# Eight PSUM banks shared out anew between scores, transposes and dense products, with P's products a step later

## The chip, the cores and the metric

The kernel runs on one core of a Trainium2 chip. A time is the device time of one execution in microseconds; fewer is better. TensorE (PE in the profile, with its weight loads as PEld) writes its products into PSUM, whose eight banks hold 128 x 512 numbers of 32 bits each; VectorE (DVE), ScalarE (ACT) and GpSimd (POOL) work beside it, SyncE (SP) issues most DMAs. Engines run their own streams and wait for one another through semaphores.

## The reference

Two layers on 1024 tokens of width 1024. Each has 16 attention heads of three kinds side by side, then a SwiGLU block and a gated per-layer input.

```python
for i in range(DEPTH):                      # DEPTH = 2
    hn = rms_norm(h, attn_norm[i])
    proj = hn @ w_in[i]                     # split into all queries, keys, values
    ...
    blocks = lax.map(lambda q0: mixer_block(q0, ...), starts)
    h = h + mix @ w_o[i]
    hf = rms_norm(h, ffn_norm[i])
    h = h + (jax.nn.silu(hf @ w_gate[i]) * (hf @ w_up[i])) @ w_down[i]
    g = jax.nn.sigmoid(rms_norm(h, ple_norm[i]) @ w_ple_gate[i])
    h = h + g * (p[i] @ w_ple_proj[i])
return rms_norm(h, final_norm)
```

`mixer_block` does for 128 queries:

```python
s = einsum('bqhd,bkhd->bhqk', q, mla_k) * scale       # 6 latent heads: causal softmax
o_mla = einsum('bhqk,bkhd->bqhd', softmax(s), mla_v)
ilog = einsum('bqhd,bkd->bqhk', idx_q, idx_k) * IDX_DIM ** -0.5
isc = einsum('bqhk,bqh->bqk', relu(ilog), idx_w)      # the indexer, 8 heads
_, sel = lax.top_k(isc, topk)                         # 256 keys for each query
...                                                   # 5 sparse heads: softmax over sel, with a bias
l1m = where(strict, log_sigmoid(-z), 0.0)             # 5 stick-breaking heads
w = where(strict, exp(log_sigmoid(z) + suffix), 0.0)
```

## The kernel before

**Tiling.** The tokens are two halves of 512. Features lie on the partitions. A dense product is 128 features by 512 tokens; every operand is a high and a low part, so each step of `gemm` (L259) over 128 inputs is three matmuls of 128x512: high by high, high by low, low by high (L266, L267, L268). ScalarE makes a weight's high part `wh` (L187), GpSimd its low part `wl` (L196).

**Two streams.** `weave` runs a main stream of dense work (in-projection, then `layer_rest`: output projection, SwiGLU, gate) and feeds a side stream, `attention(L, half)`, into it by a planned ratio. The attention of a half runs beside the dense work of the half or layer before it: (0,0) beside the in-projection's end, (0,1) beside `layer_rest(0,0)`, (1,0) beside `layer_rest(0,1)`, (1,1) beside `layer_rest(1,0)`; `layer_rest(1,1)` has nothing beside it. On TensorE instructions run in the order in which the program is written. The other engines' order is set by a scheduler by priority, with instructions that empty PSUM banks ahead.

**PSUM.** Four pools share the eight banks: `psS` (scores S, two banks to a tile, two tiles), `psT` (transposes T), `psO` (products with the values O) and `psD` (dense products D, two tiles). A tile taken again waits for the instruction that reads it last. Dense products are read by VectorE and ScalarE at L433, L508, L522, L554, L582, L616, L630, L656, L671, L1195 and L1197. T is read by L293, L344, L352, L367, L415 and by the heads' L835 and L836.

**Attention.** First the indexer: eight heads, each with a call of `scores` (L776) for every block of 128 queries (two blocks in the first half, four in the second), read by a relu on ScalarE (L1042). Then five stick-breaking heads, six latent, five sparse. While the first eleven run, VectorE also does the 32 rounds of counts of the top-k (L1082). A head has two chunks of 256 queries; a chunk of `n` pairs of key blocks runs through steps (L1122 to L1182):

- three and two steps before `s0`, `scores` of its two query blocks; in the step's second part `post_scores` reads S: two sigmoids on ScalarE (L886, L887) and a scan on VectorE (L888) for stick-breaking, VectorE's maximum (L867) and ScalarE's exp (L874) for latent, a masked maximum on VectorE (L870) for sparse;
- at `s0 + jp`, `piece(jp)`: up to four 128x128 transposes of P into T (L828); `post_piece` (L830) then has ScalarE copy T to PT's high part (L835) and VectorE subtract that for PT's low part (L836). PT has two buffers;
- a step later `pv(jp)` (L838): four matmuls of the values with PT's high and low parts into O (L845);
- after the last, `finish` (O read at L853 and L854), and at a head pair's end `norm` (L931), whose four transposes of `wide` (L941) lay the softmax row scales out in PSUM, with `scale` (L947) and `store`.

Here n is 1 and 2 in the first half (three steps to a head) and 3 and 4 in the second (seven). Within a step the order on TensorE is pv, norm, piece, scores (the table `order`), then the dense products that the ratio gives. A step's length in dense work follows from `weights`, from the number of things in it.

Of the kernel before, what the change touches and what calls it, by code (L numbers as in the profile page):

```python
# [8 lines left out]
F32 = mybir.dt.float32  # L9
# [12 lines left out]
HALF = 512  # L22
# [18 lines left out]
NORM_LATER = 1  # L41
# [6 lines left out]
STEP_W, STEPS = (4.0, 1.0), (220, 380)  # L48
SPARSE_W = 1.0
# [39 lines left out]
def trunk(ctx: ExitStack, tc, x, p, w_in, attn_norm, mla_q_norm, mla_w_uq, mla_kv_norm, mla_w_ukv,  # L89
# [5 lines left out]
    def pool(name, bufs=1, **kw):  # L95
        return ctx.enter_context(tc.tile_pool(name=name, bufs=bufs, **kw))
# [4 lines left out]
    ap = pool("ap", 1)  # L101
    sm = pool("sm", 4)
    PS = bass.MemoryType.PSUM
    psS, psT, psO, psD = pool("psS", 2, space=PS), pool("psT", 1, space=PS), pool("psO", 1, space=PS), pool("psD", 2, space=PS)
    dram = pool("dram", 1, space=bass.MemoryType.DRAM)

    def scratch(name, *shape):
# [2 lines left out]
    def S_tile():  # L110
        return psS.tile([128, 2, HALF], F32, name="S")

    def T_tile():
        return psT.tile([128, HALF], F32, name="T")

    def D_tile():
        return psD.tile([128, HALF], F32, name="D")
# [409 lines left out]
    def layer_rest(L, half):  # L527
# [179 lines left out]
                after(12 + 2 * i, lambda i=i: piece(i % 4, i // 4, T_tile))  # L707
            return
        norm.rstd()
        tiles = [S_tile()[:, i] for _ in range(2) for i in range(2)]  # L710
        tiles += [T_tile(), psO.tile([128, HALF], F32, name="O"), D_tile(), D_tile()]
        for i in range(8):
            piece(i % 4, i // 4, lambda: tiles[i])

# [1 line left out]
    def attention(L, half):  # L716
        k = (L, half)
        nk = HALF * (half + 1)
        tiles = [4 * half + i for i in range(4)]
        itiles = [t for t in tiles if t >= 2]  # L720
        off, o = {}, 0
        for t in itiles:
            off[t] = o
            o += 128 * (t + 1)
        isc = ap.tile([128, 3328], F32, name="isc")

        def have(*keys):
            return all(clock[0] - stored.get(key, 1e9) >= DELAY for key in keys)
# [47 lines left out]
        def scores(t, qs, ks, extra=None):  # L776

            n = 128 * (t + 1)
            w = max(n, 256)
            np_, w = (1, w) if w <= 512 else (2, w // 2)  # L780
            ql = (t % 4) * 128
            S = S_tile()
            for i in range(np_):
                mms = [(S[:, i, :w], a[:, ql:ql + 128], b[:, i * w:i * w + w]) for a, b in zip(qs, ks)]
                if i == np_ - 1 and extra is not None:
                    mms[1:1] = extra(t, S[:, i], n - i * w)
                for j, (o, a, b) in enumerate(mms):
                    PE.matmul(o, a, b, start=j == 0, stop=j == len(mms) - 1)  # L788
            if np_ == 1:
                return S[:, 0, :n], lambda a: a[:, :n], AX.X  # L790
            return S[:, :, :w], lambda a: a[:, :n].rearrange("p (a w) -> p a w", a=2), AX.XY

        def masked(mask):
            return lambda t, S, e: [(S[:, e - 128:e], identB, mask)]

# [9 lines left out]
        class Chunk:  # L805
# [8 lines left out]
            def scores(self, q):  # L814
                self.S[q] = scores(2 * self.c + q, *self.head.qk())
# [88 lines left out]
        class Head:  # L904
# [26 lines left out]
            def norm(self):  # L931

                j = self.i // 2
                if self.done and j in rows:
                    self.n = n = 64 if self.i % 2 == 0 else 128
                    self.S = S_tile()[:, 0]
                    wide = sm.tile([128, 4, 2, 64], F32, name="wide", bufs=1)
                    ACT.copy(wide[:, :, :n // 64], rows[j].rearrange("p h t -> p t h")[:, :, :n // 64].unsqueeze(
                        3).to_broadcast([128, 4, n // 64, 64]))
                    for t in range(4):  # L940
                        PE.transpose(self.S[:n, t * 128:(t + 1) * 128],  # L941
                                     wide[:, t, :n // 64].rearrange("p h c -> p (h c)"), identF)
# [89 lines left out]
        def indexer():  # L1032
# [27 lines left out]
            for hh in range(IDX_H):  # L1060
                qs = nxt()
                while hh + 1 < IDX_H and not have(("iq", k, (hh + 1) // 2)):
                    yield None
                for i, t in enumerate(itiles):
                    S, view, _ = scores(t, (qs, qs), (kh, kl))
                    accumulate(hh, t, S, view)
                    if i == 0 and hh + 1 < IDX_H:
                        nxt = load(hh + 1)
                    yield 0.5 + (t + 1) * 0.5
# [52 lines left out]
        post, prod = {}, {}  # L1122

        def at(d, step, f, *a):
            d.setdefault(step, []).append((f, a))

        load, first_sparse, nb = {}, None, 3 + 4 * half
        s0 = LAG[half] + 2
        for hd in heads:
            for ci, ch in enumerate(hd.chunks):  # L1130
                lag = LAG[half]
                if ci == 0:
                    at(load, s0 - lag - 2, hd.fetch)
                    at(load, s0 - lag - 1, hd.split)
                    at(load, s0 - 3, hd.fetch_values)
                    at(load, s0 - 1, hd.split_values)
                    if hd.kind is SparseHead and first_sparse is None:
                        first_sparse = s0 - lag + 1
                for q in range(2):
                    at(prod, s0 - lag + q, ch.scores, q)  # L1140
                    at(post, s0 - lag + q + 1, ch.post_scores, q)
                for jp in range(ch.n):
                    at(prod, s0 + jp, ch.piece, jp)
                    at(post, s0 + jp + 1, ch.post_piece, jp)
                    at(prod, s0 + jp + 1, ch.pv, jp)
                at(post, s0 + ch.n + 1, ch.finish)
                if ci == 1:
                    at(prod, s0 + ch.n + NORM_LATER - 1, hd.norm)
                    at(post, s0 + ch.n + NORM_LATER, hd.scale)
                    at(post, s0 + ch.n + NORM_LATER, hd.store)  # L1150
                s0 += ch.n

        order = {"finish": 0, "scale": 1, "store": 2, "post_piece": 3, "post_scores": 4, "pv": 5, "norm": 6, "piece": 7,
# [1 line left out]
        background = topk()  # L1155
        tk = TOPK_W[half] / max(first_sparse - 1, 1)
        credit = 0.0
        weights = [(STEP_W[0] + STEP_W[1] * len(prod.get(step, []))) * (1.0 if step < first_sparse else SPARSE_W) for step in range(s0 + 4)]
        unit = STEPS[half] / sum(weights)
        for step in range(s0 + 4):  # L1160
            for f, a in sorted(prod.get(step, []), key=lambda fa: order[fa[0].__name__]):
                f(*a)
            for f, a in load.get(step, []):
                while f.__name__ == "fetch" and not have(*f.__self__.needs()):
                    yield None
                f(*a)
            if step + 1 == first_sparse:
                for _ in background:
                    pass
            for f, a in sorted(post.get(step + 1, []), key=lambda fa: order[fa[0].__name__]):  # L1170
                f(*a)
            credit += tk * (TOPK_RATE[0] if step < SB_H * nb else TOPK_RATE[1])
            last = next((i for i in reversed(nc.cur_bb.bb.instructions) if i.engine == DVE.engine), None)
            with tc.issue_after(last):
                while credit > 0:
                    credit -= next(background, 1e9)
            yield weights[step] * unit
# [50 lines left out]
    def heads_of_all():  # L1228
        for L in range(DEPTH):
            for half in range(2):  # L1230
                yield from attention(L, half)
                ended.append((L, half))

    side = heads_of_all()
    parts = ((first, (), "in"), (layer_rest, (0, 0), "full"), (layer_rest, (0, 1), "full"), (layer_rest, (1, 0), "last"))
    for i, (f, a, name) in enumerate(parts):
        weave(f(*a), side, DENSE[name], ATT[i], lambda: len(ended) > i, clock)
    for _ in layer_rest(1, 1):
        pass
# [59 lines left out]
```

## Time and profile before

| | us |
|---|---|
| three runs: lowest, median, highest | 3209.86, 3210.99, 3216.07 |
| the profiled execution | 3211.26 |
| its span, first to last instruction | 3209.1 |
| attention (0,0): indexer, products with values | 56 to 99, 119 to 423 |
| attention (0,1) | 437 to 599, 627 to 1275 |
| attention (1,0) | 1292 to 1353, 1387 to 1797 |
| attention (1,1) | 1884 to 2033, 2062 to 2698 |
| top-k counts of the four | 104 to 286, 606 to 946, 1358 to 1569, 2042 to 2392 |

The mean granted clock of TensorE is 0.987. In a row of the grouped view stand line, engine, operation, output tile and inputs, shapes and count; behind the bar the busy time in total in us, the mean in ns, and the idle time of the engine just before the group in us, with the instructions that ended it. In the order of time, a row has its start and length in us, and in brackets the idle time before it.

### The profile page before, as it was taken

The page shows a single profiled execution, that of the slowest core. Times are in us where ns is not written, and L with a number is a line of the kernel's source. Part 1 is how long each engine was busy: PE and PEld are TensorE (multiplying, and loading weights), DVE is VectorE, ACT ScalarE, POOL GpSimd, SP SyncE. Part 2 cuts the span into 40 slices and gives each one's busy share as a digit, 9 for nine tenths or more (in the row PEclk, how much of TensorE's full clock was granted, in tenths as well). Part 3 has the DMA queues.
Part 4 walks back from the last instruction along what each step waited for, and adds up shares of the span by engine and source line. Part 5 has one row for each costly group of instructions (what it writes and reads, how often), then busy time and mean ns, then how long its engine had stood idle before and what let it go on. Part 6 is the DMA issues. An engine that isn't in the chain of part 4 may idle for free. (4 is left out here: it accounts for less than half of the span.)

```text
span 3209.1 us, 43576 instructions
## 1 busy us (share of the span) xinstructions
PE 3068.6 (96%) x15059; PEld 2549.1 (79%) x15059; DVE 2099.0 (65%) x3701; ACT 1486.3 (46%) x2485; POOL 1722.9 (54%) x1980
## 2 busy tenths in 40 slices
PE   8889999999998999999999999889999999999998
PEld 7768888777887888888888788767888877888877
DVE  4878656799997646687744636899997465322234
ACT  4555654445445545444444535544444455322234
POOL 4533356666445433765555744656445445766665
PEclk9999999999999999999999999999999999999999
DMA  7465453323233346433333465422333323333322
GB/s 203 117 194 147 144 172 96 91 89 96 90 97 93 105 116 176 132 103 107 107 104 89 116 162 176 116 72 86 98 97 95 89 70 113 117 99 94 98 92 73
DMA packets 549949, 363.59 MB, mean 113 GB/s; under 512 B 134672, under 2 KB 491744, under 8 KB 549728
## 3 DMA queue, kind: packets, MB, share of 16 engines
q1 hardware_dynamic: 549727, 360.81, 38.7%
q8 instruction: 119, 1.95, 0.3%
q14 instruction: 103, 0.84, 0.1%
HBM read 310.65 MB, written 50.08 MB: 112 GB/s over the span
## 5 line engine op out<-in xcount | busy, mean ns | idle before, releaser
L196 POOL TENSOR_TENSOR wl<-wr,wh 128x256 fp32r<-128x256 f32 x1684 | 1375.4, 848 | 1178.5 <-ACT wh L187 1143.9
L266 PE MATMUL D<-act,wh 128*128 128x512 f32 x3416 | 1363.6, 399 | 31.6 <-DVE h L582 16.5
L267 PE MATMUL D<-act,wh 128*128 128x512 f32 x3416 | 1341.0, 393 | 2.3 <-DVE act L633 2.0
L268 PE MATMUL D<-act,wl 128*128 128x512 f32 x3416 | 1340.0, 392 | 2.4 <-POOL wl L196 2.4
L266 PEld LDWEIGHTS D<-act,wh 128*128 128x128 f32 x3416 | 646.0, 189 | 174.7 <-issue 14.1
L268 PEld LDWEIGHTS D<-act,wl 128*128 128x128 f32 x3416 | 645.3, 189 | 145.9 <-POOL wl L196 4.8
L187 ACT CAST wh<-wr 128x1024 fp32r<-128x1024 f32 (+3 forms) x432 | 443.6, 1027 | 665.6 <-PE D L267 525.5
L267 PEld LDWEIGHTS D<-act,wh 128*128 128x128 f32 x3416 | 646.6, 189 | 126.6 <-DVE act L633 3.1
L1082 DVE TENSOR_SCALAR_CACHE_REDUCE junk<-isc,cand 128x512 uint8<-128x512 f32 (+5 forms) x396 | 371.3, 938 | 5.5
L836 DVE TENSOR_TENSOR PT<-T,PT 128x384 fp32r<-128x384 f32 (+1 forms) x320 | 201.8, 631 | 139.9 <-ACT PT L835 138.9
L835 ACT CAST PT<-T 128x384 fp32r<-128x384 f32 (+1 forms) x320 | 173.6, 542 | 192.4 <-PE T L828 181.4
L845 PEld LDWEIGHTS O<-PT,V 128*128 128x128 f32 x1280 | 196.2, 190 | 72.2 <-DVE PT L836 43.7
L845 PE MATMUL O<-PT,V 128*128 128x256 f32 x1280 | 215.5, 287 | 38.1 <-DVE PT L836 34.3
L891 POOL TENSOR_TENSOR P<-P,A 128x127 f32<-128x127 f32 (+3 forms) x80 | 101.0, 1266 | 198.3 <-DVE A L888 122.1
L788 PE MATMUL S<-kh,qh 128*128 128x384 f32 (+4 forms) x544 | 206.6, 381 | 0.3 <-ACT P L1042 0.3
L788 PE MATMUL S<-kl,qh 128*128 128x384 f32 (+4 forms) x544 | 203.8, 375 | 1.6 <-DVE kl L293 1.6
L828 PE MATMUL T<-identF,P 128*128 128x128 f32 x1152 | 182.2, 277 | 17.5 <-POOL P L891 6.6
L828 PEld LDWEIGHTS T<-identF,P 128*128 128x128 f32 x1152 | 135.4, 142 | 21.9 <-POOL P L891 9.0
L1048 DVE SCALAR_TENSOR_TENSOR isc<-P,iw,isc 128x384 f32<-128x384 f32 (+2 forms) x84 | 97.0, 1157 | 78.4 <-ACT P L1042 78.3
L619 POOL TENSOR_TENSOR tmp<-tmp,rr 128x512 f32<-128x512 f32 x88 | 120.2, 1366 | 32.4 <-DVE tmp L618 27.0
L630 DVE SCALAR_TENSOR_TENSOR tmp<-tmp,D 128x512 f32<-128x512 f32 x88 | 60.1, 683 | 107.6 <-POOL tmp L619 80.3
L853 ACT COPY o<-O 64x256 f32<-64x256 f32 x128 | 47.3, 370 | 175.4 <-PE O L845 174.0
(217 smaller groups left out, 3304.4 us busy)
## 6 DMA issues: line engine op xcount, KB each, us to landing
wr<-in_w_gate_dram SPq DMA_DIRECT2D x88, 512.0 KB, 3.8
wr<-in_w_up_dram SPq DMA_DIRECT2D x88, 512.0 KB, 3.8
wr<-in_w_down_dram SPq DMA_DIRECT2D x80, 512.0 KB, 3.4
wr<-in_w_in_dram SPq DMA_DIRECT2D x44, 512.0 KB, 3.8
wr<-in_w_in_dram SPq DMA_DIRECT2D x76, 256.0 KB, 3.8
wr<-in_w_o_dram SPq DMA_DIRECT2D x32, 512.0 KB, 4.3
wr<-in_w_ple_gate_dram SPq DMA_DIRECT2D x32, 512.0 KB, 3.8
h<-h SPq DMA_DIRECT2D x56, 256.0 KB, 4.4
```

The costliest lines, as they stand in the source:

```text
L187: ACT.copy(hi, raw)
L196: POOL.tensor_tensor(l[:, ks], a[:, ks], f32(h[:, ks]), op=ALU.subtract)
L266: PE.matmul(ps, a, ah, start=first and i == 0, stop=False)
L267: PE.matmul(ps, a, al, start=False, stop=False)
L268: PE.matmul(ps, b, ah, start=False, stop=last and i == len(ks) - 1)
L619: POOL.tensor_tensor(t, t, ffn.rep, op=ALU.mult)
L788: PE.matmul(o, a, b, start=j == 0, stop=j == len(mms) - 1)
L828: PE.transpose(ps[:, o:o + 128], self.P[q][:, j * 128:(j + 1) * 128], identF)
L835: ACT.copy(pt[:, 0, o:], self.ps[:, o:])
L836: DVE.tensor_sub(pt[:, 1, o:], self.ps[:, o:], f32(pt[:, 0, o:]))
L845: PE.matmul(self.O[:, :256], self.head.V[:, j, :], pt[:, s, o:o + 256], start=j == 0 and s == 0, stop=j == 2 * self.n - 1 and s == 1)
L1082: DVE.tensor_scalar(junk[:, :n], isc[:, off[t]:off[t] + n], c[:, i:i + 1], None, op0=op, op1=ALU.add, accum_out=cnt[:, i:i + 1])
```

## The change

One pair of S banks instead of two, two T banks instead of one, three D banks instead of two; O keeps its one. In the first half an attention takes the S pair once and holds it, and each call of `scores`, which there needs one bank, uses the pair's two banks in turn (`S_banks`); in the second half a call takes the pair as before. The head's row scales are laid out in a T tile instead of S. `pv`, `finish`, `norm`, `scale` and `store` come one step later, so an attention has one step more. The output's last eight pieces take their banks in another division. From L732 on, a line's number in the changed kernel is 9 higher.

```diff
-    psS, psT, psO, psD = pool("psS", 2, space=PS), pool("psT", 1, space=PS), pool("psO", 1, space=PS), pool("psD", 2, space=PS)
+    psS, psT, psO, psD = pool("psS", 1, space=PS), pool("psT", 2, space=PS), pool("psO", 1, space=PS), pool("psD", 3, space=PS)
...
-        tiles = [S_tile()[:, i] for _ in range(2) for i in range(2)]
-        tiles += [T_tile(), psO.tile([128, HALF], F32, name="O"), D_tile(), D_tile()]
+        S = S_tile()
+        tiles = [S[:, 0], S[:, 1], T_tile(), T_tile(), psO.tile([128, HALF], F32, name="O"), D_tile(), D_tile(), D_tile()]
...
+        if half == 0:
+            own, uses = S_tile(), [0]
+
+        def S_banks():
+
+            if half:
+                return S_tile()
+            uses[0] += 1
+            return own[:, uses[0] % 2:uses[0] % 2 + 1]
...
-            S = S_tile()
+            S = S_banks()
...
-                    self.S = S_tile()[:, 0]
+                    self.S = T_tile()
...
-                    at(prod, s0 + jp + 1, ch.pv, jp)
-                at(post, s0 + ch.n + 1, ch.finish)
+                    at(prod, s0 + jp + 2, ch.pv, jp)
+                at(post, s0 + ch.n + 2, ch.finish)
                 if ci == 1:
-                    at(prod, s0 + ch.n + NORM_LATER - 1, hd.norm)
-                    at(post, s0 + ch.n + NORM_LATER, hd.scale)
-                    at(post, s0 + ch.n + NORM_LATER, hd.store)
+                    at(prod, s0 + ch.n + NORM_LATER, hd.norm)
+                    at(post, s0 + ch.n + NORM_LATER + 1, hd.scale)
+                    at(post, s0 + ch.n + NORM_LATER + 1, hd.store)
...
-        for step in range(s0 + 4):
+        for step in range(s0 + 5):
```

What moves on TensorE, first in a stick-breaking chunk of the second layer's second half. T_20363 is P's transposes of one piece, and PT_20374 is made from it; before, its product stands at the next step, with 18 dense matmuls between (left out but for one):

```order
L828 MATMUL T_20363<-identF_84,P_20096 128x128
L828 MATMUL T_20363<-identF_84,P_20160 128x128
...
L788 MATMUL S_20368<-kl_20262,qh_20258 128x384
L266 MATMUL D_20236<-act_19988,wh_20239 128x512
...
L845 MATMUL O_20289<-PT_20374,V_20045 128x256 x4
L828 MATMUL T_20445<-identF_84,P_20096 128x128
```

Now, at such a place, with T_20311 and PT_20322 made from it, the preceding piece's product (PT_20257) and the next piece's transposes (T_20359) come in between:

```order
L837 MATMUL T_20311<-identF_84,P_20145 128x128
L837 MATMUL T_20311<-identF_84,P_20212 128x128
...
L797 MATMUL S_20316<-kl_20075,qh_20071 128x448
...
L854 MATMUL O_20193<-PT_20257,V_19887 128x256 x4
L837 MATMUL T_20359<-identF_84,P_20145 128x128
...
L797 MATMUL S_20364<-kl_20075,qh_20071 128x512
...
L854 MATMUL O_20434<-PT_20322,V_20254 128x256 x4
L837 MATMUL T_20439<-identF_84,P_20145 128x128
```

The product moved behind a second stretch of dense work; 39 dense matmuls now stand between the transposes and it.

Second, the indexer's calls of scores in the first half of the first layer, two rows to a call, with the semaphores of other engines that a row waits for (Activation is ScalarE); dense matmuls lie between the calls. Before, each call has a tile of its own, in two pairs of banks, and the third call is the first that waits for ScalarE:

```order
L788 MATMUL S_725<-kh_668,qh_722 128x384
L788 MATMUL S_725<-kl_669,qh_722 128x384
...
L788 MATMUL S_740<-kh_668,qh_722 128x512
L788 MATMUL S_740<-kl_669,qh_722 128x512
...
L788 MATMUL S_784<-kh_668,qh_781 128x384 [waits Activation_49]
L788 MATMUL S_784<-kl_669,qh_781 128x384
...
L788 MATMUL S_807<-kh_668,qh_781 128x512 [waits Activation_49]
```

Now all calls write the one tile S_447, in its two banks by turns:

```order
L797 MATMUL S_447<-kh_669,qh_723 128x384
L797 MATMUL S_447<-kl_670,qh_723 128x384
...
L797 MATMUL S_447<-kh_669,qh_723 128x512 [waits Activation_49]
L797 MATMUL S_447<-kl_670,qh_723 128x512
...
L797 MATMUL S_447<-kh_669,qh_780 128x384 [waits Activation_49]
L797 MATMUL S_447<-kl_670,qh_780 128x384
```

The wait for ScalarE has moved from the third call to the second.

Third, a pair of latent heads' end in the first layer's second half, where the row scales go into PSUM just ahead of a piece's transposes. Before:

```order
L941 MATMUL S_9889<-identF_84,wide_9890 128x128 x4
L828 MATMUL T_9896<-identF_84,P_9715 128x128
L828 MATMUL T_9896<-identF_84,P_9770 128x128
...
L788 MATMUL S_9901<-kh_9658,qh_9654 128x448
L788 MATMUL S_9901<-kl_9659,qh_9654 128x448
```

Now:

```order
L950 MATMUL T_9848<-identF_84,wide_9849 128x128 x4
L837 MATMUL T_9855<-identF_84,P_9618 128x128
L837 MATMUL T_9855<-identF_84,P_9678 128x128
...
L797 MATMUL S_9860<-kh_9557,qh_9553 128x512
L797 MATMUL S_9860<-kl_9558,qh_9553 128x512
```

They moved from S to T, where the piece's transposes follow at once.

More of the change, by code (lines that the diff above doesn't have):

```diff
@@ L1157, in attention @@
         credit = 0.0
-        weights = [(STEP_W[0] + STEP_W[1] * len(prod.get(step, []))) * (1.0 if step < first_sparse else SPARSE_W) for step in range(s0 + 4)]
+        weights = [(STEP_W[0] + STEP_W[1] * len(prod.get(step, []))) * (1.0 if step < first_sparse else SPARSE_W) for step in range(s0 + 5)]
         unit = STEPS[half] / sum(weights)
-        for step in range(s0 + 4):
+        for step in range(s0 + 5):
             for f, a in sorted(prod.get(step, []), key=lambda fa: order[fa[0].__name__]):
```

## The prediction

> **What bounds the kernel now.** I read the page's busy times first, then TensorE's rows grouped by line, then its waits in the stretches where VectorE is busiest, then the order of time around one wait.
>
> ```profile
> span 3209.1 us, 43576 instructions
> PE 3068.6 (96%) x15059; PEld 2549.1 (79%) x15059; DVE 2099.0 (65%) x3701; ACT 1486.3 (46%) x2485; POOL 1722.9 (54%) x1980
> ```
>
> TensorE is busy for 3068.6 of 3209.1 us, the next engine for 65%. The 140 us between are all that a new sharing of PSUM can win, save for the clock (below). The grouped rows end with the idle time ahead of a group and what ended it:
>
> ```profile
> L266 PE MATMUL D<-act,wh 128*128 128x512 f32 x3416 | 1363.6, 399 | 31.6 <-DVE h L582 16.5 <-DVE stg L508 3.8 <-DVE tmp L630 3.4
> L845 PE MATMUL O<-PT,V 128*128 128x256 f32 x1280 | 215.5, 287 | 38.1 <-DVE PT L836 34.3 <-DVE nm L872 1.6 <-DVE mix L854 1.1
> L828 PE MATMUL T<-identF,P 128*128 128x128 f32 x1152 | 182.2, 277 | 17.5 <-POOL P L891 6.6 <-DVE rr L367 2.9 <-DVE act L293 2.3
> L341 PE MATMUL T<-ones,rr 128*128 128x1 f32 x160 | 20.7, 250 | 11.5 <-DVE rr L323 6.9 <-DVE PT L836 4.6
> L413 PE MATMUL T<-identF,stg 128*128 128x128 f32 x96 | 15.0, 280 | 4.5 <-DVE PT L836 2.9 <-DVE stg L433 1.6
> L1188 PE MATMUL D<-identF,act 128*128 128x128 f32 x64 | 13.7, 346 | 10.1 <-DMA act<-in_x_dram 7.3 <-DVE stg L522 1.2 <-ACT h L1195 1.0
> L360 PE MATMUL T<-identF,rstd 128*128 128x128 f32 x80 | 12.6, 281 | 10.1 <-DVE rstd L352 8.2 <-DVE PT L836 1.9
> L941 PE MATMUL S<-identF,wide 128*128 128x128 f32 (+1 forms) x96 | 14.4, 272 | 0.0
> ```
>
> The costliest wait is of the products with the values (O) for PT, P's transposed copy; next is a dense product (D) for the instruction that still reads its bank (h, stg, tmp); then transposes (T), partly for the last reader of the one T bank. These are the three things that the change touches. Two stretches in which VectorE also does the top-k counts, and their shares (columns: us, busy time of PE, PEld, DVE, ACT, POOL, then granted clock, DMA share, GB/s):
>
> ```profile
> PE O L845 <- DVE PT L836: 11.8, 10, 3.1
> PE D L266 <- DVE h L582: 4.9, 4, 2.3
> PE D L266 <- DVE tmp L630: 2.1, 1, 2.1
> ...
> PE O L845 <- DVE PT L836: 20.0, 14, 3.9
> PE T L360 <- DVE rstd L352: 8.2, 1, 8.2
> PE D L266 <- DVE h L582: 3.2, 2, 1.9
> ...
> 600.00:700.00 100.00, 91.17 (x451) 75.06 (x450) 99.09 (x154) 48.56 (x70) 61.58 (x62) 0.98 0.30 92
> 700.00:800.00 100.00, 93.01 (x479) 77.12 (x478) 99.03 (x154) 50.97 (x75) 63.67 (x63) 1.00 0.31 95
> 2100.00:2200.00 100.00, 92.00 (x452) 76.22 (x451) 92.32 (x143) 49.31 (x73) 57.48 (x58) 0.95 0.28 85
> 2200.00:2300.00 100.00, 94.80 (x486) 78.95 (x485) 96.81 (x163) 48.92 (x75) 55.24 (x58) 0.98 0.31 93
> 2900.00:3000.00 100.00, 99.81 (x441) 82.35 (x440) 26.03 (x36) 25.40 (x30) 64.93 (x80) 1.00 0.32 95
> ```
>
> The first three wait rows are of 600 to 960 us, the next three of 2040 to 2440: in the second alone lie 20.0 of the 38.1 us before O. Where no attention runs (2900 to 3000) TensorE is full at 99.81 of 100.
>
> **The change part by part.** No instruction is added or removed; banks and one step of time move.
>
> *The products a step later.* The dearest wait in order of time:
>
> ```profile
> 2119.99 3.38 DVE L888 TENSOR_TENSOR_SCAN A<-A,zeros 128x1024 f32<-128x1024 f32 x1
> ...
> 2121.78 0.49 PE L828 MATMUL T<-identF,P 128*128 128x128 f32 x3
> 2124.18 0.39 PE L266 MATMUL D<-act,wh 128*128 128x512 f32 x1
> 2124.41 0.39 PE L267 MATMUL D<-act,wh 128*128 128x512 f32 x1
> 2125.54 0.28 PE L845 MATMUL O<-PT,V 128*128 128x256 f32 x1
> 2128.48 0.54 DVE L836 TENSOR_TENSOR PT<-T,PT 128x384 fp32r<-128x384 f32 x1
> 2129.08 0.62 PE L845 MATMUL O<-PT,V 128*128 128x256 f32 x3 [3.27 <-DVE PT L836]
> ...
> 2131.21 0.63 PE L267 MATMUL D<-act,wh 128*128 128x512 f32 x1
> 2131.64 0.63 PE L268 MATMUL D<-act,wl 128*128 128x512 f32 x1
> 2134.32 0.64 PE L845 MATMUL O<-PT,V 128*128 128x256 f32 x4
> ```
>
> The transposes end at 2122.3, the dense work between is used up by 2125.54, and the subtraction that makes PT's low part is held up behind a scan and other VectorE work until 2129.02. A step later the product stands where the next one does now: 2134.32, or 2131.05 without the 3.27 us of wait. That is 2.0 us behind the subtraction. So this wait goes, with a margin shorter than the wait was. In the second half the example of the change's order has 39 dense products where 18 stood, about 9 us of cover against 4. I take all of O's 38.1 us but the 1.1 that waits for `mix` (O's own bank, still one, still one step): **37**.
>
> *A third D bank.* Then a product waits for the reader of the bank three products back. By the trace each such reader had ended at least 0.5 us before its bank would come round in the old order. Of L266's 31.6 us the row names 23.7, all readers of D; I leave 2.4 out for what it doesn't name, and add 2.8 of L1188 (10.1 less 7.3 for the DMA): **32**.
>
> *A second T bank.* The waits for PT (4.6 + 2.9 + 1.9), for stg (1.6, which reads the bank as well) and L828's but for P (17.5 - 6.6 = 10.9) are for T's reader; with two banks the trace leaves 1.6 us of margin at the closest. I count the first three and the last: **20**. What waits for data stays: rr L323 6.9, rstd 8.2, P 6.6, the DMA 7.3. Together 37 + 32 + 20 = 89.
>
> *The clock.* Behind the wait at 2129 the dense products start 0.43 us apart where 0.23 was usual before it (2131.21 to 2131.64; 2124.18 to 2124.41). The granted clock there:
>
> ```profile
> 2131.00:2133.50 2.50, 2.50 (x7) 1.92 (x7) 2.50 (x7) 0.63 (x1) 0.93 (x2) 0.50 0.63 179
> 2425.00:2427.00 2.00, 2.00 (x6) 1.71 (x6) 1.46 (x2) 0.38 (x1) 0.00 (x0) 0.50 0.00 0
> 2422.78 0.62 PE L845 MATMUL O<-PT,V 128*128 128x256 f32 x3 [1.87 <-DVE PT L836]
> ```
>
> About 3.4 us at 0.50 lose 1.7 us; ten such stretches stand behind waits counted above, and since part of a stretch falls on the wait itself I take 1.2 us each: **12** more.
> [...]
>
> *One pair of S banks.* This costs. In the second half a call of scores now waits for the reader of the call just before:
>
> ```profile
> 82.00 0.33 PE L788 MATMUL S<-kh,qh 128*128 128x384 f32 x1
> 84.08 0.48 PE L788 MATMUL S<-kh,qh 128*128 128x512 f32 x1
> 86.06 0.62 ACT L759 CAST qh<-qraw 128x512 fp32r<-128x512 f32 x1 [4.78 <-DMA qraw<-iq]
> 86.59 0.49 ACT L1042 ACTIVATE P<-S 128x384 f32<-128x384 f32 x1
> ...
> 912.31 1.01 ACT L874 ACTIVATE P<-S,nm 128x896 f32<-128x896 f32 x1 [4.42 <-DVE nm L867]
> 913.33 0.48 PE L788 MATMUL S<-kh,qh 128*128 128x512 f32 x1
> ```
>
> The last two rows are one of the closest: read out at 913.32, next call at 913.33. Over the second half's calls one of 192 comes out late, by 0.3 us, and four more are within 0.5. In the first half two single banks take turns, but the order of the change shows a wait for ScalarE already at the second call: the two halves of one held tile are not told apart. The first four rows show what that costs: the call at 84.08 would wait for the relu of the call at 82.00, which stands behind a cast that waits for a DMA, until 87.08: 3.0 us. Such a wait moves later calls too, and so spares them. Put end to end, 12 of 218 calls (both halves, as far as two calls stand apart) are late by 17.3 us; letting each wait move the rest leaves about 6. I take 7, and 3 of clock: **-10** (3 to 25, the upper end being 17 and as much clock as five stretches).
>
> *The head's row scales through T.* Their 96 transposes (L941), four to a head's end, so 24 times, hold one of T's two banks for some 3 us; this gives T back one bank of slack at those places. I take **-2** of the T gain (0 to -8, where each would cost a third of a us).
>
> *What VectorE takes back.* From 600 to 800 us VectorE is busy 198.1 of 200 us. TensorE can't get ahead there by more than those 1.9 us and one step's slack, some 5 us; of the 13 us that would go there I give back 6, and 2 from 2200 to 2300: **-8**. Beyond that a new order throws up waits of its own, such as nm L872's 1.6 or mix's 1.1 now; four of about 1: **-4**.
>
> Sum: 89 + 12 - 10 - 2 - 8 - 4 = **77 us**, against the profiled execution's 3211.26 (span 3209.1; the median of the runs, 3210.99, is the same within 0.01%): **3134 us**.
>
> **The rivals.**
>
> *VectorE sets the pace in the top-k stretches.* Then the extra step fills, the subtraction comes as late as ever against it, and the waits move but do not shrink. What stays is what the two stretches hold: 11.8 + 4.9 + 2.1 + 20.0 + 3.2 = 42. The gain is 89 - 42 + 5 (clock) - 10 = 42 us, **3169**. For it: 99% from 600 to 800, 97% from 2200 to 2300. Against: VectorE averages 65%, the dearest waits of the second stretch lie where it is at 92%, and the waits there come from instructions that are out of turn (a 3.38 us scan), which a step's slack absorbs.
>
> *One pair of S banks becomes the bound: slower.* Each of the some 350 calls of scores now needs its predecessor's reader, VectorE's max then ScalarE's exp. If these came about 3 us later than now (ScalarE's casts for the weights and PT stand in the same queue), shifting every read-out against the next call gives 193 us of waits for 17; at 1 us later it is 41, at 2 us 95. The gain of 89 + 12 is eaten up from just over 2 us on. At 3 us: 3211 - 101 + 193 = **3303**. For it: the 0.0 us of margin at 913. Against: the median margin in the second half is 3 to 6 us, and nothing is added to ScalarE.
> [...]
>
> *It doesn't do what it says.* Half the gain hangs on PT being made no later than now. If VectorE's scheduler puts the subtraction back by the step that it was given, O's 37 stay and, with the S cost, 89 - 37 - 24 + 3 = 31 us remain: **3180**. If D's and T's readers slide likewise, all is given back: **3211**.
>
> **How the numbers follow.** The forecast, 3134, has 0.68 (3105 to 3155: the S term at its ends, the give-backs gone or doubled, clock 5 to 20). VectorE's pace, 3169, has 0.20; the subtraction put back, 3180, 0.04; nothing, 3211, 0.03; slower, 3303, 0.05. The range reaches from 3105 to 3178, across the second case, and leaves the last three out, and a little below. About 0.2%, 6.4 us, is what a measurement of this kernel can tell from no change: faster 0.92, same 0.03, slower 0.05.
>
> **What would show it.** Right: the waits of O for PT under 5 us, those of D for h, stg and tmp under 5, T's for PT gone, a granted clock of 0.991 or more, waits of S for ScalarE of 5 to 15 us, most of them before 100 us and in the first half. VectorE's pace: O's waits for PT still 20 or more between 600 and 960 and 2040 and 2440, VectorE at 97% or more there. The slower case: TensorE's rows for S with 50 us or more ahead of them. The prediction fails if the readers of S slide by over 2 us, or if a queue that I took as unchanged (ScalarE's casts of PT, weights) falls behind.

## The result, and the profile after

3180.39 us against 3210.43: the ratio of the runs is 0.9906, with a 95% interval from 0.9891 to 0.9920. The change gains 30 us (26 to 35); 77 were forecast, and the time lies 2 us above the range. The profiled execution's span went from 3209.1 to 3179.6 us.

TensorE's grouped rows of the changed kernel, the ones that answer to those shown of before (a line's number is 9 higher from L732 on):

```profile
L266 PE MATMUL D<-act,wh 128*128 128x512 f32 x3416 | 1362.4, 399 | 12.9 <-DVE stg L508 3.9 <-ACT act L632 2.4 <-DVE rtmp L351 2.2
L268 PE MATMUL D<-act,wl 128*128 128x512 f32 x3416 | 1343.3, 393 | 8.3 <-POOL wl L196 8.2
L797 PE MATMUL S<-kh,qh 128*128 128x384 f32 (+4 forms) x544 | 207.7, 383 | 10.3 <-ACT P L1051 3.9 <-ACT P L883 3.6 <-ACT P L896 2.5
L854 PE MATMUL O<-PT,V 128*128 128x256 f32 x1280 | 207.5, 285 | 8.8 <-DVE mix L863 8.8
L837 PE MATMUL T<-identF,P 128*128 128x128 f32 x1152 | 183.1, 275 | 24.4 <-POOL P L900 22.7 <-DVE PT L845 1.7
L341 PE MATMUL T<-ones,rr 128*128 128x1 f32 x160 | 21.6, 256 | 16.5 <-DVE rr L323 12.3 <-DVE inc L1105 4.2
L360 PE MATMUL T<-identF,rstd 128*128 128x128 f32 x80 | 12.5, 280 | 13.7 <-DVE rstd L352 13.7
...
PE 3061.0 (96%) x15059; PEld 2558.2 (80%) x15059; DVE 2100.2 (66%) x3701; ACT 1480.7 (47%) x2485; POOL 1728.2 (54%) x1980
```

Most of the waits that were to go have gone: O for PT 34.3 to 0, T for PT 9.4 to 2.6, D for h and tmp 19.9 to 2.0. D's waits for stg stayed (3.8 and 3.9). The S pair costs 10.3 us of waits, about as much as was expected of it. But other waits grew: the transposes wait for P itself (6.6 to 22.7), O for its bank (mix, 1.1 to 8.8), the norms' sums and transposes for rr and rstd (15.1 to 26.0), dense products for wl (2.4 to 8.2), and the norms' sums 4.2 us behind the top-k's `inc`. Some 55 us came back, S's 10 among them.

Where the time went is seen by numbering the dense matmuls (L266 to L268, the same 10440 in the same order in both traces) and comparing when the same one starts:

| dense matmul | before, us | after, us | ahead by |
|---|---|---|---|
| 1567th | 533.2 | 528.0 | 5.2 |
| 2872nd | 962.2 | 955.8 | 6.4 |
| 6265th | 1964.6 | 1943.6 | 21.0 |
| 7570th | 2429.2 | 2402.1 | 27.1 |
| last | 3191.7 | 3161.1 | 30.6 |

Between the first two and between the next two lie the top-k counts of the second halves, and nearly all of the 31.8 us (of 34.3) that the prediction's rows show O waiting for PT. There the change took away 40 of the 42 us of waits that the prediction counts, and gained 1.2 and 6.1 us: TensorE's idle time, added up over the two stretches, was 22.6 and 38.3 us and is 19.6 and 37.5. Three quarters of the gain come from elsewhere.

Three windows there (columns as in the prediction's windows):

```profile
600.00:700.00 100.00, 91.50 (x450) 75.15 (x449) 98.98 (x156) 47.18 (x69) 63.10 (x63) 0.97 0.29 84
700.00:800.00 100.00, 91.52 (x468) 75.07 (x467) 99.22 (x152) 49.27 (x74) 66.52 (x62) 1.00 0.32 95
...
2100.00:2200.00 100.00, 91.85 (x476) 75.75 (x475) 99.08 (x155) 48.88 (x75) 60.29 (x62) 1.00 0.33 99
```

VectorE is busy 99% in all three. TensorE is hardly fuller than it was (91.17, 93.01 and 92.00, the last at a clock of 0.95 where it is now 1.00). Between 2100 and 2200 VectorE was at 92.32 before, but the changed kernel is 21 to 27 us ahead there. Beside the same dense matmuls the kernel before had VectorE at 95%, 101.09 of 106.40 us:

```profile
2120.60:2227.00 106.40, 96.56 (x478) 80.26 (x477) 101.09 (x158) 49.72 (x76) 61.99 (x63) 0.95 0.31 94
```

The longest wait for P in order of time, with what VectorE and GpSimd do ahead of it:

```profile
627.24 2.82 DVE L897 TENSOR_TENSOR_SCAN A<-A,zeros 128x1024 f32<-128x1024 f32 x1
627.88 4.57 POOL L196 TENSOR_TENSOR wl<-wr,wh 128x256 fp32r<-128x256 f32 x3
630.26 0.64 PE L854 MATMUL O<-PT,V 128*128 128x256 f32 x4
630.73 0.27 PE L837 MATMUL T<-identF,P 128*128 128x128 f32 x1
631.89 0.56 DVE L845 TENSOR_TENSOR PT<-T,PT 128x384 fp32r<-128x384 f32 x1
632.41 1.99 POOL L900 TENSOR_TENSOR P<-P,A 128x1023 f32<-128x1023 f32 x1
634.46 0.55 PE L837 MATMUL T<-identF,P 128*128 128x128 f32 x3 [3.45 <-POOL P L900]
```

The product at 630.26 runs without a wait: a step later its PT is long made. TensorE goes straight on to the next transposes, which are of a P that isn't made yet, and waits 3.45 us for it. P's scan leaves VectorE at 630.06, but GpSimd, which makes P from the scan, is at work on wl until 632.4, so 2.2 us of this wait are GpSimd's. In eight of the 13 waits for P GpSimd starts 0.14 us behind the scan's end, and it is VectorE that comes late. The rows of one of them:

```profile
2181.57 2.28 DVE L897 TENSOR_TENSOR_SCAN A<-A,zeros 128x1024 f32<-128x1024 f32 x1
2183.06 0.64 PE L854 MATMUL O<-PT,V 128*128 128x256 f32 x4
2184.00 1.99 POOL L900 TENSOR_TENSOR P<-P,A 128x1023 f32<-128x1023 f32 x1 [4.62 <-DVE A L897]
2186.05 0.55 PE L837 MATMUL T<-identF,P 128*128 128x128 f32 x3 [2.24 <-POOL P L900]
```

Had GpSimd been free at each scan's end, an estimated 5.0 of the 22.7 us would be gone. The subtraction of before and the scan of now stand in the same queue of VectorE; TensorE had been held up by one and is held up in the main by the other.

### The profile page after: what moved, and what is told of

Its sections match the earlier page's. It is cut to its first block, busy times and chain, and to the rows that moved or that the text cites. A ratio compares the mean times of both kernels' runs of the same rounds, so it can differ in the third digit from the quotient of the medians.

```text
span 3179.6 us, 43533 instructions
## 1 busy us (share of the span) xinstructions
PE 3061.0 (96%) x15059; PEld 2558.2 (80%) x15059; DVE 2100.2 (66%) x3701; ACT 1480.7 (47%) x2485; POOL 1728.2 (54%) x1980
## 5 line engine op out<-in xcount | busy, mean ns | idle before, releaser
L266 PE MATMUL D<-act,wh 128*128 128x512 f32 x3416 | 1362.4, 399 | 12.9 <-DVE stg L508 3.9
L268 PE MATMUL D<-act,wl 128*128 128x512 f32 x3416 | 1343.3, 393 | 8.3 <-POOL wl L196 8.2
L268 PEld LDWEIGHTS D<-act,wl 128*128 128x128 f32 x3416 | 646.6, 189 | 152.9 <-POOL wl L196 11.9
L266 PEld LDWEIGHTS D<-act,wh 128*128 128x128 f32 x3416 | 647.5, 190 | 139.6 <-DVE stg L508 5.1
L797 PE MATMUL S<-kh,qh 128*128 128x384 f32 (+4 forms) x544 | 207.7, 383 | 10.3 <-ACT P L1051 3.9
L854 PE MATMUL O<-PT,V 128*128 128x256 f32 x1280 | 207.5, 285 | 8.8 <-DVE mix L863 8.8
L837 PE MATMUL T<-identF,P 128*128 128x128 f32 x1152 | 183.1, 275 | 24.4 <-POOL P L900 22.7
L883 ACT ACTIVATE P<-S,nm 128x128 f32<-128x128 f32 (+3 forms) x116 | 79.5, 686 | 122.0 <-DVE nm L876 121.6
L616 DVE TENSOR_TENSOR tmp<-D,rr 128x512 f32<-128x512 f32 x88 | 60.5, 687 | 101.5 <-PE D L268 98.2
```

The lines of the kernel that those rows point to most:

```text
L266: PE.matmul(ps, a, ah, start=first and i == 0, stop=False)
L268: PE.matmul(ps, b, ah, start=False, stop=last and i == len(ks) - 1)
L837: PE.transpose(ps[:, o:o + 128], self.P[q][:, j * 128:(j + 1) * 128], identF)
L854: PE.matmul(self.O[:, :256], self.head.V[:, j, :], pt[:, s, o:o + 256], start=j == 0 and s == 0, stop=j == 2 * self.n - 1 and s == 1)
```

## The experiments

Theory A: where O's waits lay, VectorE is full, so a step more of slack moves the wait and does not shorten it. Theory B: the one S pair takes back what the step gains. C and D, which say that the step's own order or P's short lag is to blame, are told with their runs.

**Parts alone.** First only the step on the banks of before:

```diff
-                    at(prod, s0 + jp + 1, ch.pv, jp)
+                    at(prod, s0 + jp + 2, ch.pv, jp)
...
-        for step in range(s0 + 4):
+        for step in range(s0 + 5):
```

(finish, norm, scale and store move by a step as in the change).

> Only the products' step of the change; banks as before (two S pairs, one T, two D). Theory A (VectorE sets the pace beside the top-k: a wait that goes from the products comes back ahead of the transposes of P): O's waits for PT fall from 34 us to under 5, waits of T for P or PT rise by 15 us or more, and the time is 3 to 12 us below before, no gain between 600 and 960. Theory B (the single S pair takes back what the step gains): without it the step's full 30 to 40 us show.

3236.67 us, ratio 1.0077 (1.0064 to 1.0090): 25 us slower. Its rows:

```profile
L845 PE MATMUL O<-PT,V 128*128 128x256 f32 x1280 | 205.3, 283 | 0.0
L828 PE MATMUL T<-identF,P 128*128 128x128 f32 x1152 | 182.5, 277 | 49.6 <-DVE PT L836 23.3 <-POOL P L891 6.6 <-POOL wl L196 6.0
L266 PE MATMUL D<-act,wh 128*128 128x512 f32 x3416 | 1369.5, 401 | 39.7 <-DVE h L582 20.0 <-DVE tmp L630 8.0 <-ACT act L292 1.9
```

O's waits are gone to the last tenth, and T's for the same subtraction are there instead, 23.3 us. In order of time:

```profile
2147.67 0.63 PE L845 MATMUL O<-PT,V 128*128 128x256 f32 x4
2148.14 0.47 ACT L835 CAST PT<-T 128x384 fp32r<-128x384 f32 x1
2151.72 0.55 DVE L836 TENSOR_TENSOR PT<-T,PT 128x384 fp32r<-128x384 f32 x1
2152.33 1.11 PE L828 MATMUL T<-identF,P 128*128 128x128 f32 x4 [4.02 <-DVE PT L836]
```

With one T bank the next transposes must wait for the instruction for which the product had waited. A expected the move and a small gain; the move came, the gain did not, and S, with both pairs back, can't be to blame: B falls. This run alone doesn't show A, since here it is the one T bank that sends the wait back. D's waits grew by 8 us as well and others by less. Half of the loss, 13.5 us, comes ahead of the 1567th dense matmul, where the kernel before had only 1.9 us of O's waits for PT. Over the whole run TensorE is idle for 17 us more, and stretches at half clock cost 14 us more (56.5 us, counted as in the last section). Why the step brings these, and so costs time by itself, stays open.

The other part alone, the banks with the products at the old step (the diff shown with the change, without its last two pieces):

> Only the banks of the change (one S pair, two T, three D); the products' step as before. Theory A: D's and T's waits for bank readers go as in the change, O's waits for PT stay at 25 to 40 us, and the time is 10 to 25 us below before. Theory B: within 8 us of before, with S's waits at 10 us or more and later starts behind them.

3177.34 us, ratio 0.9887 (0.9874 to 0.9901), 36 us below before and no slower than the whole change. Counted by dense matmuls as above, it gains 1.2 and 5.5 us in the two stretches, where the whole change has 1.2 and 6.1.

```profile
L266 PE MATMUL D<-act,wh 128*128 128x512 f32 x3416 | 1363.5, 399 | 9.5 <-DVE stg L508 2.9 <-ACT act L632 2.5 <-ACT act L292 2.3
L854 PE MATMUL O<-PT,V 128*128 128x256 f32 x1280 | 216.8, 288 | 40.3 <-DVE PT L845 38.1 <-DVE mix L863 1.0 <-ACT PT L844 0.9
L837 PE MATMUL T<-identF,P 128*128 128x128 f32 x1152 | 181.1, 276 | 7.4 <-POOL P L900 6.2 <-ACT stg L415 1.2
```

O waits 38.1 us for PT, P's wait is at its old 6.2. So the banks make the gain, and the step trades O's 38 us for P's and the rest, about one for one. The size was better than A's 10 to 25.

**Less work for VectorE.** The counts of the top-k read the first 128 numbers of a row instead of all, with a rank of 32 instead of 256, in the kernel before, the changed one, and the banks alone. Another selection of keys comes out; each engine has as many instructions as before, and VectorE's busy time falls from 2099 to 1910 us (250 less had been expected).

```diff
-                    DVE.tensor_scalar(junk[:, :n], isc[:, off[t]:off[t] + n], c[:, i:i + 1], None,
+                    DVE.tensor_scalar(junk[:, :128], isc[:, off[t]:off[t] + 128], c[:, i:i + 1], None,
...
-            DVE.tensor_scalar(inc, cnt, float(TOPK), None, op0=ALU.is_ge)
+            DVE.tensor_scalar(inc, cnt, 32.0, None, op0=ALU.is_ge)
```

> The kernel before, with each top-k count over the first 128 numbers of a row only (and a rank of 32 in place of 256), so VectorE has some 250 us less to do and the selection is another one. The base for the next run. Theory A: 20 to 50 us below before, with O's waits for PT in the top-k stretches under half of their 32 us. Theory B says nothing of this run.

> The changed kernel with the same light counts. Theory A: with VectorE's load gone the waits of T for P fall from 23 us to under 8, and the sum of the gains from the change and from the light counts is reached or passed: 40 us or more below the changed kernel. Theory B (one S pair): the waits for S stay at 10 us, and what the change gains over the kernel before with the same light counts is 30 us or less.

> The banks alone (one S pair, two T, three D; products at the old step) with the light counts of the two runs before; beside e6_after_light_counts it gives what the step is worth when VectorE has room. Theory A (the step's gain is lost because VectorE is full where O's waits lie): the step is worth something here, so this run is 12 to 30 us slower than e6 (3125 to 3143), and has 15 us or more of O's waits for PT. Theory C (the step loses its gain by its own order, at the heads' ends and in P's chain, whatever VectorE has to do): within 6 us of e6 (3107 to 3119).

| counts | before | banks alone | whole change | the change gains | of it the step |
|---|---|---|---|---|---|
| full | 3210 to 3214 | 3177.34 | 3180.39 | 30 | -3 |
| light | 3168.73 | 3134.47 | 3112.78 | 56 | 22 |

The ratios to the kernel before are 0.9868 (0.9853 to 0.9883), 0.9757 (0.9739 to 0.9774) and 0.9688 (0.9674 to 0.9701) for the light row. The step alone, with the same instructions, is worth 22 us where VectorE has room, intervals well apart, and nothing that can be told where it has none. Counted by dense matmuls, the profiled executions differ by 8.2 and 15.7 us in the two stretches and by under 2 us elsewhere. C, by which the step would lose its gain through its own order, expected 6 at most. Rows of TensorE's waits in the banks alone and, second, in the whole change, both light:

```profile
PE O L854 <- DVE PT L845: 24.7, 16, 4.5
PE T L837 <- POOL P L900: 5.1, 2, 2.6
```

```profile
PE T L341 <- DVE rr L323: 15.5, 7, 4.5
PE T L837 <- POOL P L900: 7.6, 4, 2.6
```

24.7 us of O's waits go (no row is left of them), and P's grow by 2.5 only; with full counts 38.1 went and 16.5 came at P alone. One stretch of the two kernels, the changed one second:

```profile
700.00:800.00 100.00, 95.12 (x490) 80.06 (x491) 77.56 (x168) 51.04 (x76) 62.12 (x65) 0.98 0.31 93
```

```profile
700.00:800.00 100.00, 100.00 (x528) 84.48 (x527) 81.50 (x177) 54.89 (x84) 68.00 (x69) 1.00 0.32 95
```

With VectorE at 78 to 82% TensorE fills up there; from 600 to 700 and from 2100 to 2200 VectorE is at 85 to 88%. The light counts are shorter instructions as well as a smaller load, and these runs don't tell which of the two sets the step's gain free. One expectation was missed: in the kernel before with light counts O's waits in the two stretches fell from 32 only to 19.5 (5.2 and 14.3), not under half. Part of them, then, does not hang on the counts' load; that it is a matter of turn, the subtraction standing behind other work in the queue, is argued from the rows above and not shown by itself. A step's slack takes this part away: with light counts no wait of O for PT is left in the changed kernel.

**P earlier.** The scores one step earlier in the second half of the changed kernel:

```diff
-LAG = (3, 3)
+LAG = (3, 4)
```

> The changed kernel with the scores one step earlier in the second half (LAG 4 in place of 3), so P has a step more. Theory A (VectorE's work itself is the bound between 600 and 800 and 2100 and 2300): T's waits for P fall from 23 us to under 8, but as much comes back elsewhere and the time is within 8 us of the changed kernel (3172 to 3188). Theory D (only P's lag is short): the waits go for good and the time is 3155 to 3170.

3184.98 us, ratio 0.9912 (0.9894 to 0.9930): no better than the change. The waits of T for P fell from 22.7 to 0.4, and these, 8.8 and 8.2 us in the change, have grown in their place:

```profile
PE O L854 <- DVE mix L863: 20.6, 9, 6.1
PE D L268 <- POOL wl L196: 16.4, 10, 3.7
```

D falls. Given slack at P, TensorE waits for `mix`, the next thing that VectorE has to do, and for wl. Four of the waits for wl, 11.8 us of the 16.4, stand behind a P that GpSimd takes up less than 0.2 us after VectorE's scan. This is theory A in its plainest form: three orders of the same work (products early, products late, scores early as well), three places of waiting, and 3177 to 3185 us.

**The counts elsewhere.** A stretch exists in which TensorE waits less: beside the latent heads. From 800 to 1000 us the changed kernel has VectorE at 92 and 94% and TensorE at 97 and 95%. The rate of the counts against their mean, beside the stick-breaking and the latent heads:

```diff
-TOPK_RATE = (1.1, 1.2)
+TOPK_RATE = (0.8, 1.25)
```

> The changed kernel with the top-k counts spread: 0.8 of the mean rate beside the stick-breaking heads and 1.25 of it beside the latent ones (before 1.1 and 1.2). Theory A: VectorE falls below 97% between 600 and 800 and its work moves to 900 to 1060, T's waits for P fall to under 12 us and the time is 5 to 20 us below the changed kernel. Theory C or D: within 5 us of it.

> The banks alone, products at the old step, with the counts spread in the same way. Theory A: O's waits for PT fall by 10 us or more and the time is 5 to 20 us below the banks alone (3157 to 3172); if the step pays once VectorE has room, it is slower than the run before this by some us. Theory C: within 5 us of 3177.

> The kernel before with the counts spread (0.8 and 1.25 of the mean rate). Beside e7 (3153.6) and e10 (3156.1) it tells what the change and its banks are worth when VectorE is less full in the stick-breaking heads. Theory A: this run is 10 to 25 us below before, and the whole change is then worth 35 to 50 us in place of 30.

> The changed kernel with the counts spread less, 0.9 and 1.15. Theory A: between the changed kernel and e7, 3153 to 3172.

> The changed kernel with the counts spread further, 0.7 and 1.3. Theory A: what counts take from the first stretch they add to the second, where the wait of the norm's transposes for rstd (10.6 us at 998 in e7) grows; within 6 us of e7 (3148 to 3160).

> The changed kernel with the counts at 0.6 and 1.4 of the mean rate, a step past 0.7 and 1.3 (3145.4). Theory A, VectorE's work only shifted: the stick-breaking heads gain less and less and the latent ones begin to pay, so 3138 to 3150, within 6 us of the run before on either side. If it is over 3152, the spread has passed its best.

| rates | kernel | us | ratio to before (95%) |
|---|---|---|---|
| 0.8, 1.25 | before | 3191.96 | 0.9941 (0.9922 to 0.9959) |
| 0.8, 1.25 | banks alone | 3156.11 | 0.9826 (0.9811 to 0.9840) |
| 1.1, 1.2 | the change | 3180.39 | 0.9906 (0.9891 to 0.9920) |
| 0.9, 1.15 | the change | 3162.85 | 0.9851 (0.9831 to 0.9870) |
| 0.8, 1.25 | the change | 3153.64 | 0.9818 (0.9801 to 0.9835) |
| 0.7, 1.3 | the change | 3145.37 | 0.9790 (0.9773 to 0.9806) |
| 0.6, 1.4 | the change | 3138.50 | 0.9769 (0.9756 to 0.9783) |

The changed kernel gets faster at every step of the spread, by 42 us at the last, where it is 74 us below the kernel before: a version that beats both. The gains at 0.8 and at 0.7 were larger than expected. Counting dense matmuls as above, the 0.8 run gains 23.9 us in the first of the two stretches and 26.8 in the second, where the change had 1.2 and 6.1. Two stretches of the last run:

```profile
700.00:800.00 100.00, 98.53 (x515) 82.67 (x514) 94.39 (x137) 51.87 (x80) 70.28 (x66) 1.00 0.34 100
...
900.00:1000.00 100.00, 86.27 (x433) 71.68 (x433) 98.94 (x190) 47.67 (x82) 40.88 (x46) 0.92 0.31 90
```

From 700 to 800 TensorE does 98.53 us where it did 91.52; the price is paid from 900 to 1000, where VectorE is now at 98.94 and TensorE at 86, not 95. At 0.8 and 1.25 the change gains 38 us on the same spread of the kernel before, and the banks alone 36: VectorE is still 97% busy beside the stick-breaking heads there, and the step is still worth nothing that can be told. The changed kernel at those rates:

```profile
600.00:700.00 100.00, 96.44 (x494) 79.88 (x493) 97.24 (x141) 56.42 (x81) 70.46 (x67) 1.00 0.32 95
700.00:800.00 100.00, 98.25 (x517) 82.65 (x516) 96.56 (x154) 52.23 (x79) 68.56 (x69) 1.00 0.32 95
```

That share is now of a TensorE that does 96 and 98 us of work in the same time, not 91 and 92.

## Why the prediction was wrong

- **The step that failed is "the products a step later": 37.** The rule read off the trace was right as far as it went: the subtraction ended at 2129.02, the later product would come at 2131.05, and O's waits went to 0. What it took as given is that everything else that VectorE owes TensorE would be as early as before with TensorE ahead. In those stretches VectorE had little time left; the gain there was 7 us where the sum had 34 (42 less the give-back of 8). The term measures -3 alone on top of the banks, 22 with light counts.
- **"What VectorE takes back", -8 and -4 for new waits**, was mis-sized: new waits other than S's are about 45 us, some 31 of them in the two stretches. The bound was read from 600 to 800, with 2 us given back for 2200 to 2300. VectorE's 92% from 2100 to 2200 was taken as room; beside the dense matmuls of that window of the changed kernel it was 95%, and it rose to 99.08.
- **The rival "VectorE sets the pace" was the right mechanism**, at a chance of 0.20. It forecast 3169 and that O's waits for PT would stay at 20 us or more; they went, others came in their place, for P above all, and 11 us more were lost. The case "It doesn't do what it says" named 3180, which is the measured time, but by luck: in it O's 37 us were to stay.
- **D's third bank, 32, and T's second, 20**: with the -10 for S and the -2 for the row scales that is 40, plus clock; the banks alone gave 36. The mechanism held and the size nearly. D's third bank won more than S lost with its second pair: D's waits for h and tmp fell by 17.9 us, those of S came to 10.3. D's readers kept 5.9 us in the whole change (3.9 for stg), and the norms' waits for rr, which are for data, rose from 6.9 to 12.3.
- **S, -10**: 10.3 us of waits, where the term had 7, and 3 of clock. That the size came out is in part luck, for the place did not: 3.3 us lie in the first halves' attentions, where most were expected, and 6.6 in the second halves', where 0.3 had been read off. The wait for the other bank of one held tile is there: a relu ends at 75.32, and the next call, into the other bank, starts at 75.37.

```profile
74.84 0.48 ACT L1051 ACTIVATE P<-S 128x384 f32<-128x384 f32 x1
75.37 0.50 PE L797 MATMUL S<-kh,qh 128*128 128x512 f32 x1 [1.93 <-ACT P L1051]
```

- **The clock, +12**: nothing. The stretch from which the term was read is in the trace of before: in the four windows of 1 us from 2130 to 2134 the granted clock was 0.77, 0.50, 0.50 and 0.52, 1.7 us lost. No run shows the gain, nor the 5 us of clock that stand at the low end of the range and in VectorE's pace; what the profiled executions show is 42 us lost to stretches at 0.50 before and 51 after (counted as in the last section). The mean granted clock is 0.984 in the profiled execution and 0.986 and 0.987 in the others (0.987 before): stretches at 0.50 stand at new waits too, such as the one for P that ends at 634.46 (3.45 us; 0.50 from 636 to 638) and the one for wl that ends at 2228.06 (4.13 us; 0.50 from 2228 to 2233). From 2000 to 2100 it fell from 0.93 to 0.90, about an 11.0 us wait for rstd (8.2 before). With light counts, where the rows of TensorE's waits add up to 71 us instead of 114, it is 0.992.

```profile
2000.00:2100.00 100.00, 82.97 (x388) 67.77 (x387) 88.73 (x137) 50.93 (x72) 61.15 (x58) 0.90 0.26 73
```

## What to carry to other kernels

In this kernel a wait of the busiest engine for another engine could be slid away only where the other one had time to spare in that stretch; at 95 to 99% busy a later consumer only met the next thing in the same queue. Read the waited-for engine's share stretch by stretch, and count the waits inside a full stretch at nothing, not at half: here 40 of 42 us of them went, and 7 were gained. More banks paid where the bank's reader was only a little late: D's 22 waits for h and tmp were 2.3 us at most, and the banks alone gained 36 us. Where an engine is full, try first to move its background work to another stretch: the spread of the counts alone gained the changed kernel 42 us, more than the whole change had.

## What the runs showed of the hardware

From before to after the clock's loss did not follow the idle time. TensorE's idle time fell by 22 us (136.7 to 114.4), but the time lost to stretches at 0.50, half their length added up over the profiled execution's clock record, did not fall: it was 42 us and is 51. By the granted clock of the changed kernel's other three executions, 0.986 and 0.987, it is an estimated 41 to 45 us. In either trace there are 14 waits of 1.8 to 2.7 us outside such stretches; with eight a stretch began during the wait or at most 2.91 us behind its end, with six none did for 15 us. One of the eight of before is the 1.87 us wait at 2422.78, with the clock at 0.50 from 2425.00 to 2427.00. What tells the eight from the six these runs don't show. Behind the only wait over 0.4 us between 434 and 631 in the changed kernel, 2.39 us long, the clock stood at 0.50.

```profile
614.78 0.69 PE L837 MATMUL T<-identF,P 128*128 128x128 f32 x3 [2.39 <-POOL P L900]
...
615.20:618.40 3.20, 3.20 (x11) 2.41 (x10) 3.13 (x7) 1.82 (x3) 2.74 (x4) 0.50 0.00 0
```
